# Hybrid backbone on one core: a score product of 128 rows instead of 64, and row statistics issued four chunks together

## The chip, the core and the metric

The kernel runs on one core of a Trainium2 chip. The metric is device time in microseconds (us) of one execution. TensorE (PE) multiplies; its weight loads are shown as an engine of their own, PEld, because they may run beside the products. VectorE (DVE), ScalarE (ACT) and GpSimd (POOL) work element by element, SyncE (SP) starts most transfers. Each engine works through its own queue in order and waits on semaphores for the others. Products write into PSUM, of which this kernel holds five buffers: three wide ones (tag "w", 1024 columns) and two narrow ones (tag "m", 512 columns).

## What is computed

Two layers over 512 latent tokens and 256 context tokens of width 1024. Cut to what matters here:

```python
def rmsnorm(x, g):
    return x * rsqrt(mean(x * x, -1) + EPS) * g

def attend(q, k, v):                       # 4 heads; q, k: 128 columns without and 64 with rotary position
    s = einsum('bqhd,bkhd->bhqk', q, k) * ATTN_SCALE
    return einsum('bhqk,bkhd->bqhd', softmax(s), v)

def layer(xl, xc, ...):                    # latent stream xl, context stream xc
    h = modulate(rmsnorm(x, norm1_g), ...)
    ...                                    # gated MLP, recurrent mixer, attention, concatenated
    x = x + g1 * (concat @ w_out)
    h2 = modulate(rmsnorm(x, norm2_g), ...)
    x = x + g2 * ec_moe(h2)                # 16 experts; each takes its top rows by softmax(h2 @ w_router)

out = rmsnorm(xl, final_norm_g)            # after two layers
```

The context stream gets no output in the second layer, so there the statistics and the experts work on the latent rows alone.

## The kernel before, in words

X holds both streams with the width on the partitions: 8 chunks (k or m) of 128, 512 latent columns (s = 0) and 256 context columns (s = 1). Each layer runs `mixer` (lines 533 to 1036) and then `moe`. The code is written in dependency order; a scheduler sets the order of each engine's queue from priorities when the program is built, so instructions of neighbouring steps interleave.

**Precise products.** A float32 operand that is to be exact is split into a high and a low part in the one-pass format fp32r, and `mm3` (lines 265 to 268) multiplies high by high, low by high and high by low. A product with plain float32 operands runs as two passes (two weight loads and two matmuls in the trace).

**Attention.** Per layer two head pairs p; `scores(h, qt)` computes one tile of 128 queries by 768 keys (256 keys for a context query) in PSUM, in segments of 512 and 256 columns, and for each segment five products: `mm3` on the 128 position-free rows, and two on the rotary rows (lines 963 and 964). `krs[0]` and `krs[1]` hold the high and low part of the rotary key, the 64 rows twice. `qr[h]` holds the high part of head h's rotary query in 64 rows and its low part in the other 64. Line 963 multiplies all 128 rows by `krs[0]`; line 964 takes the 64 high rows alone, by `krs[1]`. Then DVE takes the row maximum (L967), ACT the exponential (L970), DVE the division (L972), PE transposes the result (L985), ACT and DVE split it (L273, L274), and `values` multiplies it by V.

**Row statistics.** The sum of squares over the width is a product with a column of ones, the router's logits one with the router's weights; both have 32 output rows. Chunk k writes PSUM rows 32g to 32g + 31, g = k % 4: one of four column tiles of the PE array. In `Stats.add` (lines 408 to 417), called by `out_tiles` after each update of X (L885), ACT squares the chunk (L411), and PE at once issues two products: router weights by X (L414) and ones by the square (L415), both float32. `Stats.gain` (L423) scales X for the expert rows on ACT. `Ssq` does the same for sums of squares alone (L372): at the start, for the two low-rank norms and at the end of the first layer's experts. `finish` does it for the output (L1184).

**From the statistics to the experts.** `route` copies the sums (L440, L441), turns the four row groups into one column per token (L444), takes the inverse root on DVE, the softmax, and then the top rows of each expert on DVE in rounds of eight (L496, L497, L500), while PE transposes the rows (L477) that ACT scales and SP writes to memory. An indirect gather (L1060) brings the first expert's rows back, and `moe` starts (L1104 in the first layer, L1091 in the second).

**Weights.** `Stream` loads all weights in a fixed order into slots as these come free; a load is issued when the last reader of a slot is done. Six large slots open when the early part of the mixer is over (`early_done`).

Of the kernel before, what the change touches and what calls it, by code (L numbers as in the profile page):

```python
# [7 lines left out]
F32 = mybir.dt.float32  # L8
# [10 lines left out]
TT = T + C  # L19
# [157 lines left out]
def tile_hybrid_backbone(ctx: ExitStack, tc: tile.TileContext, xT, ctxT, cc, cols, fin, w_mod, w_in, w_uq, w_ukv,  # L177
# [181 lines left out]
    class Ssq:  # L359


        def __init__(self, psp, n, nk):
            self.ps, self.n, self.nk = psp.tile([128, 1024], F32, tag="w", name="ssqps"), n, nk

        def add(self, k, src, o, tmp):
            n = src.shape[1]
            sq = tmp()[:, 0]
            act.activation(sq[:, :n], src, AF.Square)
            g = k % 4
            for a in range(0, n, 512):  # L370
                e = min(n, a + 512)
                pe.matmul(self.ps[32 * g:32 * g + 32, o + a:o + e], ones, sq[:, a:e], start=k < 4,  # L372
                          stop=k + 4 >= self.nk)

        def rstd(self, psp, dim, tmp):

# [11 lines left out]
    class Stats:  # L388


        def __init__(self, l, psp, pl):
            self.ps = psp.tile([128, 1024], F32, tag="w", name="stps")
            self.l, self.xa, self.wr = l, ([], []), []
            for s in range(1 if l == L - 1 else 2):
                w = pl.tile([128, KD, 32], F32, tag=f"wr{s}", name=f"wr{s}", bufs=1)
                pool.memset(w, 0.0)
                dve.tensor_mul(w[:, :, :E], wrt[:, l], bcast(A2[l][:, :, s:s + 1], [128, KD, E]))
                self.wr.append(w)
            self.cb = []
            for s in range(len(self.wr)):  # L400
                ps = psp.tile([128, 512], F32, tag="m", name="cb")
                for k in range(KD):
                    pe.matmul(ps[:, :E], bcast(MOD[l][:, SH2 + k, s:s + 1], [128, 128]), wrt[:, l, k], start=k == 0,
                              stop=k == KD - 1)
                self.cb.append(small.tile([128, E], F32, name="cb"))
                dve.tensor_copy(self.cb[s], ps[:, :E])

        def add(self, s, k, tmp, half):
            o, n = SEG[s]
            sq = tmp()[:, 0, :n]  # L410
            act.activation(sq, X[:, k, o:o + n], AF.Square)  # L411
            g = k % 4
            ps = self.ps[32 * g:32 * g + 32, o:o + n]
            pe.matmul(ps, self.wr[s][:, k], X[:, k, o:o + n], start=k < 4, stop=False)  # L414
            pe.matmul(ps, one_e, sq, start=False, stop=k >= 4)  # L415
            if k < KD - 2:
                self.gain(s, k, half)

        def gain(self, s, k, half):

# [112 lines left out]
    def mixer(l, U, psp, rstd, hs):  # L533
# [340 lines left out]
        def out_tiles(key, sub, m0, nm, sg, mh, ml, stats=None):  # L874
            i, wh, wl = S.take(*key, sub)
            nk = wh.shape[1]
            for s, (o, n) in sg:
                for m in range(nm):
                    c = m * 128
                    ps = psp.tile([128, 512], F32, tag="m", name="ops")  # L880
                    for k in range(nk):
                        mm3(ps[:, :n], wh[:, k, c:c + 128], wl[:, k, c:c + 128], mh[k][:, o:o + n], ml[k][:, o:o + n],
                            k == 0, k == nk - 1)
                    xs = X[:, m0 + m, o:o + n]
                    dve.scalar_tensor_tensor(xs, ps[:, :n], MOD[l][:, G1 + m0 + m, s:s + 1], xs, op0=OP.mult,  # L885
                                             op1=OP.add)
# [26 lines left out]
        for p in range(2):  # L913
# [41 lines left out]
            def scores(h, qt):  # L955
                q = slice(qt * 128, (qt + 1) * 128)
                ctx_q = qt * 128 >= T
                ps = psp.tile([128, 1024], F32, tag="w", name="sps")
                r = slice(h * 64, (h + 1) * 64)
                for ko, kn in SEG[1:] if ctx_q else SEG:  # L960
                    c = slice(ko, ko + kn)
                    mm3(ps[:, c], qh[h][:, q], ql[h][:, q], kh[h][:, c], kl[h][:, c], True, False)
                    pe.matmul(ps[:, c], qr[h][:, q], krs[0][:, c], start=False, stop=False)
                    pe.matmul(ps[:, c], qr[h][r, q], krs[1][r, c], start=False, stop=True)
                k0 = T if ctx_q else 0
                mx = small.tile([128, 4], F32, name="mx", bufs=4)
                dve.reduce_max(mx[:, 0:1], ps[:, k0:TT], axis=AX.X)  # L967
# [50 lines left out]
                fills(fl["o1"][p][sub])  # L1018
        rt = [route(l, s, stats, psp, half, tmp, hs) for s in range(len(segs))]
        if full:  # L1020
            next(rt[0])
            Pc = [[scores(h, 4 + i2) for i2 in range(2)] for h in range(2)]
            next(rt[0])
            for h in range(2):
                values(h, 2, Pc[h])
# [3 lines left out]
                out_tiles(("o1", l, 1, 1), sub, 4 * sub, 4, sg_all[1:], ych, ycl, stats)  # L1029
            for _ in rt[0]:  # L1030
                pass
        next(rt[-1])
        mods(fl["route"], psp, ahead=0)
        for _ in rt[-1]:
# [11 lines left out]
    def moe(l, P, psp, last, hs):  # L1046
# [1 line left out]
        M = CAP_L if last else CAP_L + CAP_C  # L1048

        def tmp():  # L1050
            return P.tile([128, 1, T if last else TT], F32, tag="sq" if last else "xst", name="tmp", bufs=3 if last else 4)

        gcol, gidx, sidx, gleft = picks[l]

# [105 lines left out]
        def finish(src):  # L1160
# [3 lines left out]
            slots = [S.raw.pop(0) for _ in range(4)]  # L1164
            xf, ot = [[q.tile([128, 4, 512], F32, tag=t, name=t, bufs=1) for q, t in slots[2 * i:2 * i + 2]]
                      for i in range(2)]
            first = [t[:, c] for t in tm for c in (slice(512), slice(512, 1024))]

            def turn(m, dst):
# [4 lines left out]
            def after(m):  # L1174
# [5 lines left out]
                    act.activation(f, xs, AF.Copy, scale=fint[:, m:m + 1])  # L1180
                else:
                    pool.tensor_scalar(f, xs, fint[:, m:m + 1], None, op0=OP.mult)
                g = m % 4
                pe.matmul(sq_ps[32 * g:32 * g + 32, :512], ones, sq, start=m < 4, stop=m >= 4)  # L1184
                if m < 4:
                    turn(m, first)

# [42 lines left out]
        def flush(e):  # L1230
# [10 lines left out]
            elif e == E - 3:  # L1241
                add_rows(0, lat(E // 2 - 2))
            elif e == E - 1:
                ssq = Ssq(psp, TT, KD)
                for s, src in ((0, lat(E // 2 - 1)), (1, [(YE.pop(("c", e // 4)), 8 + e // 4)])):
                    o, n = SEG[s]
                    add_rows(s, src, lambda m: ssq.add(m, X[:, m, o:o + n], o, tmp))
# [145 lines left out]
```

## Time and profile before

| | |
|---|---|
| median of three runs | 1968.45 us (1968.11 to 1972.2) |
| the profiled execution, its own time | 1967.79 us |
| its span in the trace | 1966.0 us |
| PE busy | 1795.0 us (91%) |
| DVE, ACT, POOL busy | 709.2, 482.1, 80.6 us |
| transfers | 506.52 MB, 258 GB/s on average |

The span lies 1.8 us below the profiled execution's time, and that lies 0.66 us below the median. In a view by windows each row is a stretch of the span with the busy time and count of each engine, the granted PE clock as a share of full speed, the busy share of the transfer engines and GB/s. In the chain of waits each row is a piece of the chain that ended last: its start, its length, engine, tile and line; the recorded chain begins at 468.92 us, so for the first layer's mixer the timeline stands in. A matmul's row in the timeline gives its start and length; consecutive matmuls overlap, so what one costs is read from start to start.

### The profile page before, as it was taken

To read this page: it belongs to the slowest core of one execution; us is meant where nothing else is said; L and a number is where in the kernel's file an instruction comes from. 1 tells how busy PE (TensorE), PEld (TensorE's weight loads), DVE (VectorE), ACT (ScalarE), POOL (GpSimd) and SP (SyncE) were. 2 spreads that over 40 slices of the span, in tenths; PEclk is the share of its full clock that TensorE was granted. 3 is DMA by queue.
4 is the path that set the end of the run, shared out by engine and by line. 5 is a ranking of instruction groups with operands and counts; after the bars stand their busy time and mean duration, and the time that the engine had idled before them with its cause. 6 is when DMAs were issued, how large, how long until landed. Compare 5 with 4: busy or idle time off the path is not lost.

```text
span 1966.0 us, 37614 instructions
## 1 busy us (share of the span) xinstructions
PE 1795.0 (91%) x16777; PEld 1066.6 (54%) x16777; DVE 709.2 (36%) x1479; ACT 482.1 (25%) x839; POOL 80.6 (4%) x95
## 2 busy tenths in 40 slices
PE   7999999996999999999999898999968797887896
PEld 5877778753666566556555686777522232222322
DVE  6456556634111321321322747666331020210213
ACT  4354233442111121121112455244311010010002
POOL 0000000004000000000000000000130000000001
PEclk9999999997999999999999899999979999999998
DMA  9233322226999799799694223322499999999994
GB/s 322 110 131 127 130 87 88 108 93 234 354 386 389 271 395 383 274 389 386 266 366 152 99 108 110 113 77 87 178 330 391 402 398 398 407 389 403 409 409 158
DMA packets 132338, 506.52 MB, mean 258 GB/s; under 512 B 11472, under 2 KB 13392, under 8 KB 124368
## 3 DMA queue, kind: packets, MB, share of 16 engines
q1 hardware_dynamic: 123744, 473.61, 63.1%
q0 software_dynamic: 8288, 30.41, 4.5%
q8 instruction: 132, 2.16, 0.4%
q14 instruction: 30, 0.25, 0.0%
q10 hardware_dynamic: 144, 0.09, 0.0%
HBM read 496.74 MB, written 7.34 MB: 256 GB/s over the span
## 4 chain that ended last, share of the span: by engine, by line
PE 55%; DMA 16%; DVE 3%; ACT 1%; issue 0%; POOL 0%; POOLq 0%; ACTq 0%; DVEq 0%
PE gps L1104 9%; PE ups L1104 9%; PE dps L1104 8%; DMA rawB<-in_w_up 6%; PE cps L1220 4%; PE gps L1091 3%; DMA rawB<-in_w_down 3%; PE ups L1091 2%; DMA rawA<-in_w_down 2%; PE dps L1091 1%; PE inps L266 1%; PE inps L267 1%; PE inps L268 1%; DMA splA<-in_w_up 1%; DMA rawA<-in_w_up 1%; PE ttp L1080 1%
## 5 line engine op out<-in xcount | busy, mean ns | idle before, releaser
L1287 DVE TENSOR_TENSOR hd<-sg,ups 128x768 f32<-128x768 f32 (+1 forms) x32 | 26.3, 821 | 355.5 <-PE ups L1091 202.4
L1104 PE MATMUL dps<-rawB,hdt 128*32 128x256 f32 x1824 | 122.5, 379 | 0.6 <-ACT hdt L1121 0.6
L1104 PE MATMUL gps<-rawB,xst 128*32 128x256 f32 x1584 | 118.4, 380 | 0.0
L266 PE MATMUL inps<-hh,splA 128*128 128x512 f32 (+1 forms) x296 | 106.1, 360 | 5.2 <-ACT splA L133 4.2
L1104 PE MATMUL ups<-rawB,xst 128*32 128x256 f32 x1488 | 105.4, 380 | 0.0
L267 PE MATMUL inps<-hh,splA 128*128 128x512 f32 (+1 forms) x296 | 104.0, 352 | 1.2 <-DVE splA L134 1.2
L268 PE MATMUL inps<-hl,splA 128*128 128x512 f32 (+1 forms) x296 | 103.1, 352 | 0.2 <-DVE hl L601 0.2
L1091 PE MATMUL gps<-rawB,xst 128*64 128x512 f32 x312 | 83.4, 613 | 10.7 <-DMA rawB<-in_w_gate 10.6
L1223 DVE SCALAR_TENSOR_TENSOR X<-cps,mod,X 128x512 f32<-128x512 f32 (+1 forms) x112 | 73.7, 673 | 47.7 <-PE cps L1220 46.6
L1137 ACT ACTIVATE yel<-dps,gcol 64x768 fp32r<-64x768 f32 x16 | 14.3, 894 | 309.6 <-PE dps L1104 309.6
L134 DVE TENSOR_TENSOR splA<-rawA,splA 128x1024 fp32r<-128x1024 f32 (+3 forms) x58 | 65.4, 1138 | 68.3 <-ACT splA L133 67.8
L1091 PE MATMUL ups<-rawB,xst 128*64 128x512 f32 x304 | 76.5, 601 | 14.1 <-DMA rawB<-in_w_up 14.1
L1104 PEld LDWEIGHTS dps<-rawB,hdt 128*32 128x32 f32 x1824 | 67.2, 110 | 39.8 <-ACT hdt L1121 0.8
L1278 ACT ACTIVATE sg<-gps 128x768 f32<-128x768 f32 (+1 forms) x32 | 22.5, 704 | 266.5 <-PE gps L1091 145.3
L1104 PEld LDWEIGHTS gps<-rawB,xst 128*32 128x32 f32 x1584 | 57.7, 110 | 38.8 <-issue 6.9
L133 ACT ACTIVATE splA<-rawA 128x1024 fp32r<-128x1024 f32 (+3 forms) x58 | 56.3, 988 | 91.0 <-PE ops L268 47.0
L885 DVE SCALAR_TENSOR_TENSOR X<-ops,mod,X 128x512 f32<-128x512 f32 (+1 forms) x72 | 47.5, 661 | 82.7 <-PE ops L268 82.7
L1091 PE MATMUL dps<-rawB,hdt 128*64 128x512 f32 x296 | 69.7, 599 | 5.9 <-DMA rawB<-in_w_down 5.9
L1104 PE MATMUL gps<-splA,xst 128*32 128x256 f32 x912 | 74.2, 380 | 0.0
L1104 PEld LDWEIGHTS ups<-rawB,xst 128*32 128x32 f32 x1488 | 54.5, 110 | 32.8 <-PE ttp L1124 1.2
L1138 DVE SCALAR_TENSOR_TENSOR ye<-dps,gcol,ye 64x512 fp32r<-64x512 f32 x32 | 24.0, 750 | 130.0 <-ACT ye L1137 130.0
L1138 DVE SCALAR_TENSOR_TENSOR yel<-dps,gcol,yel 64x768 fp32r<-64x768 f32 x16 | 16.1, 1009 | 149.7 <-ACT yel L1137 149.7
(356 smaller groups left out, 3530.5 us busy)
## 6 DMA issues: line engine op xcount, KB each, us to landing
rawB<-in_w_down SPq DMA_DIRECT2D x75, 1024.0 KB, 14.4
rawB<-in_w_gate SPq DMA_DIRECT2D x65, 1024.0 KB, 15.4
rawB<-in_w_up SPq DMA_DIRECT2D x64, 1024.0 KB, 14.9
rawA<-in_w_mod SPq DMA_DIRECT2D x40, 1024.0 KB, 5.0
splA<-in_w_up SPq DMA_DIRECT2D x30, 1024.0 KB, 12.1
splA<-in_w_down SPq DMA_DIRECT2D x30, 1024.0 KB, 12.8
splA<-in_w_gate SPq DMA_DIRECT2D x29, 1024.0 KB, 13.9
rawA<-in_w_up SPq DMA_DIRECT2D x26, 1024.0 KB, 11.8
```

What stands on the lines that cost most here:

```text
L133: self.nc.scalar.activation(h, src, AF.Copy)
L134: self.nc.vector.tensor_sub(l, src, h.bitcast(F32))
L266: pe.matmul(o, lh, rh, start=start, stop=False)
L267: pe.matmul(o, ll, rh, start=False, stop=False)
L268: return pe.matmul(o, lh, rl, start=False, stop=stop)
L885: dve.scalar_tensor_tensor(xs, ps[:, :n], MOD[l][:, G1 + m0 + m, s:s + 1], xs, op0=OP.mult, op1=OP.add)
L1091: pe.matmul(ps[g * 64:(g + 1) * 64, :512], lhs[:, k], w[:, g * 512:(g + 1) * 512], start=k == 0, stop=k == KD - 1)
L1104: pe.matmul(ps[32 * g:32 * g + 32, to], lhs[:, k, 32 * x:32 * x + 32], w[:, of], start=k == 0, stop=k == KD - 1)
L1138: dve.scalar_tensor_tensor(to[:, 1], ps, gate, to[:, 0].bitcast(F32), op0=OP.mult, op1=OP.subtract)
L1220: pe.matmul(ps[:, :n], y[:, hl, m * 128:(m + 1) * 128], oh[i][:, :n], start=i == 0 and hl == 0, stop=i == len(src) - 1 and hl == y.shape[1 ...
L1223: dve.scalar_tensor_tensor(xs, ps[:, :n], MOD[l][:, G2 + m, s:s + 1], xs, op0=OP.mult, op1=OP.add)
L1287: dve.tensor_mul(HD[e], sg, up)
```

## The change

The last of a score segment's five products takes all 128 rows of `qr[h]` and of `krs[1]` instead of 64 (so the low part of the query meets the low part of the key as well). `Stats.add` only squares and remembers; `emit` issues the products of the remembered chunks, first all with the router's weights, then all with ones, and is called when four are remembered, in `out_tiles` before the next update of X. For the first layer's latent rows one score tile of the context queries is put ahead of the last `emit`. `Ssq` at the end of the first layer's experts and `finish` gather four squares in the same way (the other `Ssq` keep one at a time). The experts' buffer ring for squares in the second layer has 4 places instead of 3.

```diff
         def add(self, k, src, o, tmp):
             ...
             act.activation(sq[:, :n], src, AF.Square)
-            g = k % 4
-            for a in range(0, n, 512):
-                ...
+            self.todo.append((k, sq, o, n))
+            if len(self.todo) == self.batch:
+                for k, sq, o, n in self.todo:
+                    ...
+                self.todo = []
...
         def add(self, s, k, tmp, half):
             ...
             act.activation(sq, X[:, k, o:o + n], AF.Square)
-            g = k % 4
-            ps = self.ps[32 * g:32 * g + 32, o:o + n]
-            pe.matmul(ps, self.wr[s][:, k], X[:, k, o:o + n], start=k < 4, stop=False)
-            pe.matmul(ps, one_e, sq, start=False, stop=k >= 4)
+            self.todo.append((s, k, sq))
             if k < KD - 2:
                 self.gain(s, k, half)
+
+        def emit(self):
+            at = lambda s, k: self.ps[32 * (k % 4):32 * (k % 4) + 32, SEG[s][0]:sum(SEG[s])]
+            for s, k, sq in self.todo:
+                pe.matmul(at(s, k), self.wr[s][:, k], X[:, k, SEG[s][0]:sum(SEG[s])], start=k < 4, stop=False)
+            for s, k, sq in self.todo:
+                pe.matmul(at(s, k), one_e, sq, start=False, stop=k >= 4)
+            self.todo = []
...
+                    if stats and len(stats.todo) == 4:
+                        stats.emit()
                     xs = X[:, m0 + m, o:o + n]
...
-                r = slice(h * 64, (h + 1) * 64)
...
-                    pe.matmul(ps[:, c], qr[h][r, q], krs[1][r, c], start=False, stop=True)
+                    pe.matmul(ps[:, c], qr[h][:, q], krs[1][:, c], start=False, stop=True)
...
+            Pc = [[scores(0, 4)], []]
+            stats.emit()
             next(rt[0])
-            Pc = [[scores(h, 4 + i2) for i2 in range(2)] for h in range(2)]
+            for h, qt in ((0, 5), (1, 4), (1, 5)):
+                Pc[h].append(scores(h, qt))
...
+        stats.emit()
         next(rt[-1])
...
-                g = m % 4
-                pe.matmul(sq_ps[32 * g:32 * g + 32, :512], ones, sq, start=m < 4, stop=m >= 4)
+                sqs.append(sq)
+                if m % 4 == 3:
+                    for g in range(4):
+                        pe.matmul(sq_ps[32 * g:32 * g + 32, :512], ones, sqs.pop(0), start=m == 3, stop=m == 7)
...
-                ssq = Ssq(psp, TT, KD)
+                ssq = Ssq(psp, TT, KD, batch=4)
```

In the attention the order of the queues stays as it was. It moves where statistics are taken. PE, second layer, last output product: `ops` are its products, `stps` the statistics (L414 with the router's weights, L415 with ones; in the changed kernel these are L425 and L427). Before, a piece from its middle:

```order
L414 MATMUL stps<-X,wr_13074 32x512
L268 MATMUL ops<-ycl,splA_12767 128x512
L266 MATMUL ops<-ych,splA_12767 128x512
L415 MATMUL stps<-tmp,one_e 32x512
L267 MATMUL ops<-ych,splA_12767 128x512
L268 MATMUL ops<-ycl,splA_12767 128x512
L266 MATMUL ops<-ych,splA_12767 128x512
L414 MATMUL stps<-X,wr_13074 32x512
```

Now, around the first group:

```order
L268 MATMUL ops<-ycl,splA_12770 128x512
L425 MATMUL stps<-X,wr_13074 32x512 x4
L427 MATMUL stps<-tmp,one_e 32x512 x4
L266 MATMUL ops<-ych,splA_12770 128x512
L267 MATMUL ops<-ych,splA_12770 128x512
```

Single statistics between two or three output products became a block of eight. PE, the end of the same stage, before (`htp` are the transposes of the expert rows, `rpc` is the first step of `route`):

```order
L268 MATMUL ops<-ycl,splA_12770 128x512
L477 MATMUL htp<-ident,xa 128x128 x2
L415 MATMUL stps<-tmp,one_e 32x512
L477 MATMUL htp<-ident,xa 128x128 x6
L414 MATMUL stps<-X,wr_13074 32x512
L477 MATMUL htp<-ident,xa 128x128 x5
L415 MATMUL stps<-tmp,one_e 32x512
L477 MATMUL htp<-ident,xa 128x128 x3
L444 MATMUL rpc<-sel,tmp 128x17 x2
```

and now:

```order
L268 MATMUL ops<-ycl,splA_12770 128x512
L425 MATMUL stps<-X,wr_13074 32x512 x3
L488 MATMUL htp<-ident,xa 128x128
L425 MATMUL stps<-X,wr_13074 32x512
L427 MATMUL stps<-tmp,one_e 32x512 x4
L488 MATMUL htp<-ident,xa 128x128 x4
L455 MATMUL rpc<-sel,tmp 128x17 x2
```

The last group stands behind the last output product, split by one transpose; most transposes moved behind `rpc`. DVE, first layer, top rows of the latent tokens (MAX, MAX_INDEX, MATCH_REPLACE are one round) with the context's updates of X between, before:

```order
L491 COPY tk<-rpt 64x256
L496 MAX gk<-tk 64x8
L497 MAX_INDEX ix<-gk,tk 64x8
L500 MATCH_REPLACE tk<-gk,tk 64x256
L885 SCALAR_TENSOR_TENSOR X<-ops,mod_94,X 128x256
L496 MAX gk<-tk 64x8
L885 SCALAR_TENSOR_TENSOR X<-ops,mod_94,X 128x256
```

and now (the update of X is L898, the rounds are L507, L508, L511):

```order
L502 COPY tk<-rpt 64x256
L507 MAX gk<-tk 64x8
L508 MAX_INDEX ix<-gk,tk 64x8
L511 MATCH_REPLACE tk<-gk,tk 64x256
L507 MAX gk<-tk 64x8
L508 MAX_INDEX ix<-gk,tk 64x8
L511 MATCH_REPLACE tk<-gk,tk 64x256
L898 SCALAR_TENSOR_TENSOR X<-ops,mod_94,X 128x256
```

The first update of X moved one round later; after that they still alternate.

## Rows read from the trace of the kernel before

**Rows 1.** Windows by stage (start:end, length; PE, PEld, DVE, ACT, POOL; clock, DMA, GB/s).

```profile
257.00:309.00 52.00, 48.80 (x423) 36.32 (x422) 35.51 (x85) 25.11 (x55) 0.00 (x0) 0.99 0.35 122
345.00:387.00 42.00, 39.51 (x321) 29.50 (x320) 28.50 (x60) 18.74 (x37) 0.00 (x0) 1.00 0.30 107
...
399.00:429.00 30.00, 29.61 (x86) 11.27 (x85) 8.30 (x13) 11.25 (x19) 0.87 (x1) 0.98 0.22 75
...
441.00:462.00 21.00, 18.82 (x102) 10.56 (x101) 13.24 (x50) 8.81 (x21) 9.57 (x9) 0.99 0.66 230
...
483.00:1071.00 588.00, 586.98 (x9592) 342.97 (x9585) 123.16 (x207) 78.31 (x140) 13.25 (x15) 1.00 0.89 338
...
1072.00:1090.00 18.00, 16.46 (x64) 6.38 (x63) 12.65 (x21) 10.56 (x20) 0.54 (x2) 1.00 0.25 106
...
1272.00:1308.00 36.00, 34.03 (x255) 24.35 (x254) 25.56 (x51) 17.49 (x35) 0.00 (x0) 1.00 0.37 119
1343.00:1387.00 44.00, 40.38 (x275) 30.89 (x276) 28.32 (x59) 19.19 (x40) 0.76 (x1) 0.96 0.20 73
1387.00:1418.00 31.00, 31.00 (x97) 11.84 (x97) 6.43 (x9) 10.45 (x18) 3.51 (x5) 1.00 0.70 271
...
1445.00:1933.00 488.00, 418.90 (x1824) 137.15 (x1820) 72.86 (x117) 42.22 (x78) 12.44 (x14) 1.00 1.02 398
```

**Rows 2.** Line 964, its matmuls: count, ns min/median/max, first and last start, forms.

```profile
L964 PE MATMUL sps<-krs,qr x72: 379/384/502, 263.3 to 1373.9; 64*128 64x256 f32 x40, 64*128 64x512 f32 x32
```

**Rows 3.** Timeline of PE, one score tile of the second layer (start, us, engine, line).

```profile
1372.47 0.40 PE L963 MATMUL sps<-krs,qr 128*128 128x512 f32 x1
1372.80 0.49 PE L964 MATMUL sps<-krs,qr 64*128 64x512 f32 x1
1373.22 0.39 PE L266 MATMUL sps<-kh,qh 128*128 128x256 f32 x1
1373.45 0.28 PE L267 MATMUL sps<-kh,ql 128*128 128x256 f32 x1
1373.56 0.28 PE L268 MATMUL sps<-kl,qh 128*128 128x256 f32 x1
```

**Rows 4.** Chain of waits, second layer, pieces of the output product with statistics.

```profile
1402.27 0.23 PE ops L266
1402.51 0.97 PE stps L415 x2
1403.48 0.43 PE ops L267
...
1404.38 0.97 PE stps L414 x2
1405.36 0.86 PE stps L415 x2
```

**Rows 5.** Timeline, first layer: two statistics products on different column tiles.

```profile
414.32 0.62 PE L415 MATMUL stps<-tmp,one_e 128*32 128x512 f32 x1
414.33 0.62 PE L414 MATMUL stps<-X,wr 128*32 128x512 f32 x1
...
415.31 0.50 PE L267 MATMUL ops<-ych,splA 128*128 128x512 f32 x1
```

**Rows 6.** Chain of waits, first layer's experts: one product on four column tiles.

```profile
539.34 10.36 PE gps L1104 x191
```

**Rows 7.** From the page, part 5: weight loads of such a product (busy, mean ns).

```profile
L1104 PEld LDWEIGHTS gps<-rawB,xst 128*32 128x32 f32 x1584 | 57.7, 110 | 38.8 <-issue 6.9
```

**Rows 8.** Windows in and behind the second layer's last output product.

```profile
1406.00:1414.00 8.00, 8.00 (x25) 3.15 (x24) 2.25 (x3) 2.49 (x4) 0.00 (x0) 1.00 0.00 2
...
1418.00:1445.00 27.00, 8.79 (x114) 6.95 (x114) 17.19 (x76) 7.36 (x15) 14.91 (x15) 0.68 0.57 190
```

**Rows 9.** Windows of 8 us in which PE waits often, or stands nearly still.

```profile
300.00:308.00 8.00, 6.45 (x57) 5.25 (x56) 6.24 (x16) 5.49 (x14) 0.00 (x0) 1.00 0.43 135
...
1437.00:1445.00 8.00, 2.12 (x12) 1.47 (x14) 2.40 (x14) 0.86 (x2) 4.99 (x7) 0.50 0.44 116
```

More of the change, by code (lines that the diff above doesn't have):

```diff
@@ L359, in tile_hybrid_backbone, with __init__ @@
     class Ssq:
-        def __init__(self, psp, n, nk):
+        def __init__(self, psp, n, nk, batch=1):
             self.ps, self.n, self.nk = psp.tile([128, 1024], F32, tag="w", name="ssqps"), n, nk
+            self.batch, self.todo = batch, []
         def add(self, k, src, o, tmp):
@@ L368, in add @@
             act.activation(sq[:, :n], src, AF.Square)
-            g = k % 4
-            for a in range(0, n, 512):
-                e = min(n, a + 512)
-                pe.matmul(self.ps[32 * g:32 * g + 32, o + a:o + e], ones, sq[:, a:e], start=k < 4,
-                          stop=k + 4 >= self.nk)
+            self.todo.append((k, sq, o, n))
+            if len(self.todo) == self.batch:
+                for k, sq, o, n in self.todo:
+                    g = k % 4
+                    for a in range(0, n, 512):
+                        e = min(n, a + 512)
+                        pe.matmul(self.ps[32 * g:32 * g + 32, o + a:o + e], ones, sq[:, a:e], start=k < 4,
+                                  stop=k + 4 >= self.nk)
+                self.todo = []
         def rstd(self, psp, dim, tmp):
@@ L392, in __init__ @@
             self.ps = psp.tile([128, 1024], F32, tag="w", name="stps")
-            self.l, self.xa, self.wr = l, ([], []), []
+            self.l, self.xa, self.wr, self.todo = l, ([], []), [], []
             for s in range(1 if l == L - 1 else 2):
@@ L1050, in tmp @@
         def tmp():
-            return P.tile([128, 1, T if last else TT], F32, tag="sq" if last else "xst", name="tmp", bufs=3 if last else 4)
+            return P.tile([128, 1, T if last else TT], F32, tag="sq" if last else "xst", name="tmp", bufs=4)
         gcol, gidx, sidx, gleft = picks[l]
@@ L1166, in finish @@
                       for i in range(2)]
+            sqs = []
             first = [t[:, c] for t in tm for c in (slice(512), slice(512, 1024))]
```

## The prediction

> **What bounds the kernel now.** First the windows by stage [rows 1]: look at which engine fills each stretch. From 483 to 1071 us, the first layer's experts, PE is busy 586.98 of 588 us; from 1445 to 1933, the second layer's, the transfers have a share of 1.02 and PE waits for weights. Neither stretch holds an edited instruction, so what the change brings must come from the mixers, and each of these two stages then starts earlier by what stands before it. In the attention (257 to 309, 345 to 387, 1272 to 1308, 1343 to 1387) PE is busy 48.80, 39.51, 34.03 and 40.38 us, 163 of 174 us, and DVE 118 us. In the output product with statistics (399 to 429, 1387 to 1418) PE is full and DVE and ACT stay below 12 us each. PE is thus the bound of every stage that the change touches, and the next question is what a PE instruction costs there from start to start.
>
> Second, the single tile [rows 3]. A product of 256 columns is followed by the next after 0.11 us (1373.56 after 1373.45), one of 512 after 0.23, as in the chain, where such a piece is 0.23 long [rows 4]. Around line 964 the steps are longer: 0.33 up to it, 0.42 from it to the next product, and 0.23 for that one, a 256-column product. Over 0.23, 0.23 and 0.11 that is 0.10 + 0.19 + 0.12, about 0.4 us more for one product on 64 rows. There are 72 such products [rows 2].
>
> Third, the chain in the statistics [rows 4]: L415 is a piece of 0.97 us, L414 and L415 in a row 0.97 + 0.86, and the output product behind such a block takes 0.43 instead of 0.23. So the two passes of 512 columns are worth 0.86, entering costs 0.11 and leaving 0.20: a block is 1.17 us, a second product in it 0.86 more.
>
> **The change part by part.** *The score product.* Its own 72 instructions stay; the loss around them goes: 72 x 0.4 = 28 us of PE time at most, 20, 16, 16 and 16 of them in the four attention windows and four among the context's queries. Queue orders stay, so what is late next is softmax: over the four windows PE would need 163 - 27 = 136 us, DVE 118 [rows 1], 87% of PE's, and PE already waits 6.45 busy of 8 us where DVE has 6.24 [rows 9]. So each gap that closes on PE is partly opened again as a wait for DVE and ACT. Bounds: all, 28 us; a third, 9, if DVE's bursts set the pace. I take two thirds, 18.7, since over whole windows PE stays the longer one.
>
> *Statistics of the latent rows, second layer.* Sixteen products stand in 14 blocks now: 14 x 1.17 + 2 x 0.86 = 18.1 us. After, two groups of eight. That a group is cheap rests on column tiles working side by side: at 414.32 an L415 and an L414 on different tiles start 0.01 us apart, and the next output product follows 0.99 later, what one product alone costs [rows 5]; and line 1104, which sends each weight to four column tiles of 256 columns, makes 191 passes in 10.36 us, 54 ns each [rows 6], a quarter of the 0.215 that half of a 512-column pass is. So a group costs 0.11 + 0.86 + 0.86 + 0.20 = 2.03. Two groups are 4.1, and 14.0 us go. The last group comes behind the last output product: it has to wait for that product's update and square, and one transpose splits it; but the lone products that stood there had 13 transposes between them, most of which now come later, beside DVE's work on the root. I let the two cancel, and put one block, 1.2, either way into the bounds.
>
> *Whether this reaches the end.* The weights that the second layer's experts begin with must come in a shorter time. The transfers have a share of 0.70 in 1387 to 1418 [rows 1], with 8 us from 1406 in which they stand still, and 0.57 in the 27 us after it [rows 8]: 9.3 + 11.6, some 21 us idle; 14 fits. The first layer's experts have PE as their bound, so their start moves them whole.
>
> *First layer, latent rows.* The order has 14 blocks too, in one of them two column tiles at once [rows 5]: 14 x 1.17 + 0.86 = 17.2, against 2 x 2.03 = 4.1: 13.1. The score tile put ahead of the last group covers the wait for the last square; it is only moved.
>
> *First layer, context rows.* 256 columns halve the passes: a block is 0.43 + 0.31 = 0.74. Before 14 blocks and one more product, 10.8 us; the order after has three lone products, one group of three and two runs that end in four: six blocks with two second halves, 5.3. PE gives up 5.5 of its 18.82 us in the window 441 to 462, where DVE has 13.24 with the top rows [rows 1]; PE would need 13.3, and the two take turns. I take 4; bounds 1 and 5.5.
>
> *End of the first layer's experts.* Seven blocks instead of ten, some of half width, about 2.7 us of PE's 16.46 in 1072 to 1090; DVE has 12.65 there [rows 1]. I take 2, bounds 0 and 2.7. *Output.* The scheduler spreads the products of `finish` over five blocks instead of six, and one transpose group now stands ahead of four products and waits for POOL: 1 us, bounds -1 and 2, one block each way and a little.
>
> *Sum.* 18.7 + 14.0 + 13.1 + 4 + 2 + 1 = 52.8 us. 1967.8 - 52.8 = 1915.0; the profiled execution lies 0.7 below the median, so 1915.7, rounded to 1916.
>
> *A rule that speaks against it.* The Trainium skill, page "TensorE: Matmul & The Clock Gate", Part 3, "The mechanism", says that a weight load overlaps running products only when its row group differs; column tiles share all rows. What it would make of the time is a rival below.
>
> **The rivals.** *Softmax takes over* (a wait in place of the one removed). If DVE's maxima and splits set the pace, the score term shrinks to 3 to 8 us. For it: the window with 6.24 of 8 us on DVE and 6.45 on PE [rows 9]. Against: DVE's 118 of 174 us [rows 1]. With 5 us: 1929.5, about 1925 to 1933.
>
> *Column tiles run one after another.* Then a group is 8 x 0.86 + 0.31 = 7.2 and only the switches are saved: 18.1 - 14.4 = 3.7, 17.2 - 14.4 = 2.8, little elsewhere; with 18.7 for the scores 26 us, 1942. Against: [rows 5, 6].
>
> *The loads of a group stand open.* Each pass pays its weight load of 110 ns [rows 7]: 96 passes, 10.6 us, 1926. Against: 54 ns per pass at line 1104 [rows 6], half of one load. The rule of the Trainium skill on row groups would give this; the rows of line 1104 differ from it, and the measurement decides.
>
> *The transfers eat the second layer's gain.* If the slots come free no earlier, 14 and that layer's share of the scores are lost, about 23 us: 1939. Against: the idle transfers from 1406 to 1414 [rows 8].
>
> *Slower: PE's clock falls in the attention.* Where PE stood nearly still, 2.12 busy of 8 us, the granted clock was 0.50, its lower level of 1.2 GHz [rows 9]. A PE that waits more often could fall there. Each us of its work at the lower level costs one more; of 136 us of work in the four windows more than 53, some 40%, would have to run so before the kernel is slower than now; with 60% it is 1967.8 - 53 + 82 = 1997. Against: 6.45 busy of 8 us kept 1.00 [rows 9], and I expect at least that share.
>
> **How the numbers follow.** My forecast, scores 12 to 28 and the other terms within their bounds, is 1902 to 1931: chance 0.79. Softmax takes over 0.09; tiles one after another 0.02; open loads 0.03; transfers 0.03; clock 0.04. The range is 1902 to 1932, which holds most of the forecast, half of the softmax case and the open loads, 0.8 or a little over. A measurement of this kernel tells 0.2%, 4 us, from no change. Slower by more than that is the clock case, most of it: 0.03; within it 0.01; faster all else, 0.96.
>
> **What would show it.** Line 964's rows (976 after) would be 128*128 with medians like line 963's, and the steps around it 0.23 and 0.12. The statistics would stand in blocks of eight with some 2 us from start to end; 4 to 7 us would show tiles in turn. The window of the output product in the second layer would shrink from 31 to about 17 us, and the experts of both layers keep their lengths of 588 and 488. The attention windows would be 3 to 7 us shorter each, with more waits of PE for L967, L970 and L273's successors. Wrong would be the forecast if the attention kept its length, if a gather or first weight came late, or if the granted clock in the mixers fell.

## The result, and the profile after

The changed kernel takes 1911.51 us (median of four, 1908.77 to 1914.29), the kernel before 1968.28 beside it: a ratio of 0.9713, 95% interval 0.9696 to 0.973, 56.8 us. A second set of five runs gave 1915.56 us beside 1966.41, 50.9 less by the medians; its recorded ratio is 0.9719 (0.9698 to 0.9739). The profiled execution took 1910.17 us, its span is 1908.4, 57.6 less than the span before.

First the windows of the kernel after, to be set against those of before [rows 1]: start:end, length, busy time and count of PE, PEld, DVE, ACT and POOL, clock, transfer share, GB/s.

```profile
254.00:301.00 47.00, 42.35 (x428) 35.60 (x426) 35.63 (x85) 24.67 (x55) 0.00 (x0) 1.00 0.39 136
...
443.00:1037.00 594.00, 588.65 (x9600) 344.26 (x9600) 123.81 (x211) 78.65 (x141) 19.02 (x22) 0.99 0.88 336
...
1343.00:1360.00 17.00, 16.99 (x87) 10.02 (x85) 6.75 (x10) 10.62 (x18) 3.51 (x5) 1.00 1.02 404
1360.00:1387.00 27.00, 9.01 (x121) 7.57 (x122) 16.55 (x75) 6.87 (x14) 14.65 (x14) 0.74 0.69 240
1387.00:1876.00 489.00, 420.48 (x1826) 137.82 (x1826) 73.18 (x118) 42.56 (x78) 12.71 (x14) 0.99 1.02 398
```

The second layer's output product with statistics, 31 us long before, is 17 us long and just as full. The transfers that stood idle beside it are at 1.02 now, so they did start earlier. Both stages of experts keep their length (first gate product to last down product: 587.5 us in the first layer before and after).

To see where each microsecond went, the trace is cut at marks that both kernels have: first or last starts of a tile's products, as the views by tile give them. (`kps` are the products that make the keys, `pvps` those of `values`; `ops<-ych` is the output product on the attention's result, `gps` the experts' first product, `rpc` the first step of `route`.) The last two columns are two experiments, the new score product alone and the grouped statistics alone.

| stretch | before | after | scores alone | statistics alone |
|---|---|---|---|---|
| start to first score product | 257.6 | 254.7 | 254.2 | 254.7 |
| to first `ops<-ych` (first layer's first head pair) | 55.8 | 50.0 | 49.9 | 55.2 |
| to first `rpc` (second pair, output product, latent statistics) | 115.7 | 97.0 | 110.4 | 101.6 |
| to first `gps` (context rows, route) | 53.7 | 47.3 | 53.1 | 48.3 |
| to last `kps` (first layer's experts, second layer's mixer up to its second pair) | 847.8 | 841.8 | 842.7 | 849.2 |
| to last `rpc` (second pair, output product, statistics) | 88.9 | 70.1 | 84.2 | 74.6 |
| to the end | 546.5 | 547.5 | 547.4 | 548.4 |
| span | 1966.0 | 1908.4 | 1941.9 | 1932.0 |

The two halves add up: in the third line 5.3 and 14.1 make 19.4 against 18.7, in the sixth 4.7 and 14.3 make 19.0 against 18.8. A second trace of the same changed kernel has 95.4 in the third line instead of 97.0, so differences of that size between two traces say nothing. The first line holds no edit; the first `kps` product, 21 us ahead of the scores, starts between 232.1 and 236.8 us in the twelve traces of this study in which nothing ahead of it was edited. Of the 57.6 us some 3 are therefore of that kind.

The timeline of a score tile after (the same place as [rows 3]; start, us, engine, line):

```profile
1328.71 0.39 PE L975 MATMUL sps<-krs,qr 128*128 128x512 f32 x1
1328.95 0.40 PE L976 MATMUL sps<-krs,qr 128*128 128x512 f32 x1
1329.18 0.28 PE L266 MATMUL sps<-kh,qh 128*128 128x256 f32 x1
1329.30 0.28 PE L267 MATMUL sps<-kh,ql 128*128 128x256 f32 x1
```

The steps around the edited product are 0.24, 0.23 and 0.12 us, where they were 0.33, 0.42 and 0.23. The view of that line alone (count; ns min/median/max; first and last start):

```profile
L976 PE MATMUL sps<-krs,qr x72: 276/283/400, 260.2 to 1329.7; 128*128 128x256 f32 x40, 128*128 128x512 f32 x32
```

The median fell from 384 ns [rows 2] to 283, with more rows in the product.

Now a group of statistics, in the timeline of all engines:

```profile
1349.49 0.40 PE L268 MATMUL ops<-ycl,splA 128*128 128x512 f32 x1
1349.82 0.16 PEld L425 LDWEIGHTS stps<-X,wr 128*32 128x32 f32 x8 [0.37 <-issue]
1349.82 1.06 PE L425 MATMUL stps<-X,wr 128*32 128x512 f32 x8
...
1350.27 0.13 PEld L427 LDWEIGHTS stps<-tmp,one_e 128*32 128x32 f32 x4 [0.30 <-ACT tmp L416]
1350.70 1.04 PE L427 MATMUL stps<-tmp,one_e 128*32 128x512 f32 x8
...
1351.67 0.50 PE L266 MATMUL ops<-ych,splA 128*128 128x512 f32 x1
1352.01 0.40 PE L267 MATMUL ops<-ych,splA 128*128 128x512 f32 x1
```

Its sixteen passes (two for each of eight products) stand in two rows of 8. From entry (1349.82) to the next output product (1351.67) it is 1.85 us, plus 0.10 on the way in and 0.11 on the way out: 2.06, where the sum had 2.03. Before, a single product cost 1.17 [rows 4].

The second group of the second layer is not so tidy. The chain of waits after:

```profile
1356.14 0.99 PE stps L425 x6
1357.13 0.26 PE htp L488
1357.39 0.55 PE stps L425
1357.94 0.02 PE stps L427 x3
1357.96 0.41 PE stps L425
1358.37 0.86 PE stps L427 x5
```

Three products go ahead with what is ready, a transpose comes between, and the rest follows: 3.1 us instead of 1.85.

### The profile page after: what moved, and what is told of

The parts are those of the page before. It is cut to its first block, busy times and chain, and to the rows that moved or that the text cites. A ratio compares the mean times of both kernels' runs of the same rounds, so it can differ in the third digit from the quotient of the medians.

```text
span 1908.4 us, 37615 instructions
## 1 busy us (share of the span) xinstructions
PE 1736.6 (91%) x16777; PEld 1059.2 (56%) x16777; DVE 708.3 (37%) x1479; ACT 481.5 (25%) x839; POOL 80.7 (4%) x95
## 4 chain that ended last, share of the span: by engine, by line
PE 55%; DMA 17%; DVE 3%; ACT 2%; issue 1%; POOL 0%; POOLq 0%; ACTq 0%; DVEq 0%
PE gps L1120 9%; PE ups L1120 9%; PE dps L1120 9%; DMA rawB<-in_w_up 6%; PE cps L1239 4%; DMA rawB<-in_w_down 3%; DMA rawA<-in_w_down 3%; PE gps L1107 3%; PE ups L1107 3%; PE dps L1107 1%; PE inps L266 1%; PE inps L267 1%; PE inps L268 1%; DMA splA<-in_w_up 1%; DMA rawA<-in_w_up 1%; PE ttp L1096 1%
## 5 line engine op out<-in xcount | busy, mean ns | idle before, releaser
L1153 ACT ACTIVATE yel<-dps,gcol 64x768 fp32r<-64x768 f32 x16 | 14.3, 894 | 309.6 <-PE dps L1120 309.6
L1120 PEld LDWEIGHTS gps<-rawB,xst 128*32 128x32 f32 x1584 | 57.7, 110 | 38.9 <-issue 6.9
L898 DVE SCALAR_TENSOR_TENSOR X<-ops,mod,X 128x512 f32<-128x512 f32 (+1 forms) x72 | 47.5, 660 | 54.4 <-PE ops L268 54.4
## 6 DMA issues: line engine op xcount, KB each, us to landing
rawB<-in_w_up SPq DMA_DIRECT2D x64, 1024.0 KB, 14.3
rawA<-in_w_up SPq DMA_DIRECT2D x26, 1024.0 KB, 11.8
```

The lines of the kernel that those rows point to most:

```text
L1120: pe.matmul(ps[32 * g:32 * g + 32, to], lhs[:, k, 32 * x:32 * x + 32], w[:, of], start=k == 0, stop=k == KD - 1)
```

## Experiments

### The score product alone

```diff
-                    pe.matmul(ps[:, c], qr[h][r, q], krs[1][r, c], start=False, stop=True)
+                    pe.matmul(ps[:, c], qr[h][:, q], krs[1][:, c], start=False, stop=True)
```

> The kernel before with one line changed: the scores' last product takes all 128 rows. Theory (a product on 64 rows costs 0.4 us around it, and softmax hands part of that back): 72 x 0.4 = 28 us at most, the recorded term is 18.7, and the marks of the changed kernel's trace (its attention windows shorter by about 6, 5 and 10 us, some context tiles beside) point to 20 to 22: 1946 to 1950 us. Rival (softmax takes over): 3 to 8 us, 1960 to 1965. If the two halves of the change help each other, this run and the one with the statistics alone will add up to less than the whole 57 us; the theory has them independent, since they lie in different stretches.

Measured: 1944.71 us against 1966.37, ratio 0.9892 (0.9874 to 0.991), 21.7 us less. Softmax does not take over, but it takes a part back, and matched windows show it. They are the first layer's first head pair (first score product to first `ops<-ych`) and the second layer's second pair (last `kps` to last `pvps`). Before:

```profile
257.60:313.40 55.80, 52.53 (x442) 39.62 (x441) 37.91 (x89) 27.21 (x59) 0.00 (x0) 0.97 0.33 115
1330.60:1386.90 56.30, 52.67 (x346) 41.13 (x345) 34.39 (x72) 23.40 (x49) 0.76 (x1) 0.97 0.20 75
```

the first pair in the run of the next section, the changed kernel with the 64-row product put back:

```profile
254.70:309.90 55.20, 51.45 (x442) 38.16 (x442) 37.91 (x89) 27.05 (x59) 0.00 (x0) 1.00 0.33 116
```

and both in the changed kernel (the run with the scores alone has the same first pair, PE busy 44.68 of 49.9 us):

```profile
254.70:304.70 50.00, 44.82 (x441) 37.39 (x440) 37.92 (x89) 26.66 (x59) 0.00 (x0) 1.00 0.37 128
1290.80:1342.50 51.70, 47.66 (x347) 40.72 (x346) 34.02 (x72) 23.36 (x49) 0.76 (x1) 0.97 0.22 81
```

The first row of before holds more than the edit. For 3.4 us of it the granted clock was at its lower level:

```profile
307.96:311.38 3.42, 3.42 (x18) 3.42 (x17) 1.56 (x4) 1.63 (x4) 0.00 (x0) 0.50 0.30 119
```

The run with the 64-row product put back has no such fall in this stretch and is 0.6 us shorter, so it is the one to compare with. Against it PE's busy time falls by 6.6 us with 20 products, its idle time grows from 3.75 to 5.18 us, and 5.2 reach the end. In the second stretch, with 16 such products and a clock of 0.97 before and after, the busy time falls by 5.0 and the idle time grows by 0.4. Part of the new idle time in the first pair is a wait for softmax (in all, times, longest), where the same wait was 0.6 us before:

```profile
PE sps L266 <- ACT tmp L982: 2.1, 2, 1.5
```

The price itself is read better from start to start, as in [rows 3]: from the product ahead to the second product behind, less 0.2335 us for each 512 columns, the mean step of the output products in the chain. Over the 68 products of the four head pairs these steps lose 27.1 us before and 5.2 in the changed kernel. The difference is 21.8 us, and the run gave 21.7.

### The statistics alone

The changed kernel with the 64-row product put back.

> The changed kernel with the 64-row score product put back, so that the grouped statistics stand alone. Theory: 14.0 + 13.1 + 4 + 2 + 1 = 34 us below the kernel before, 1934 us; the marks of the changed kernel's trace (13.3, 14.0, about 5, 0.3, 0) say 33 to 35. Rival (column tiles one after another): 8 us, 1960. Rival (each pass pays its weight load): about 24 us, 1944. Rival (transfers take the second layer's part): 20 us, 1948.

Measured: 1934.32 us, ratio 0.9841 (0.9821 to 0.9862), 32.0 us less than before. The table splits it: 14.1 for the first layer's latent rows, 5.4 for the context rows, 14.3 for the second layer; the other stretches move by -2.9 to +1.9 us and cancel. None of the three rivals comes near.

### Is it the entry, or the product on 64 rows?

Three runs ask what the 0.4 us is paid for. In the kernel before, the 64-row product twice in a row; in the changed kernel, the 128-row product twice; and in the kernel before, the two 64-row products of a tile put next to each other.

```diff
-                for ko, kn in SEG[1:] if ctx_q else SEG:
-                    c = slice(ko, ko + kn)
+                cs = [slice(ko, ko + kn) for ko, kn in (SEG[1:] if ctx_q else SEG)]
+                for c in cs:
                     mm3(...)
                     pe.matmul(ps[:, c], qr[h][:, q], krs[0][:, c], start=False, stop=False)
+                for c in cs:
                     pe.matmul(ps[:, c], qr[h][r, q], krs[1][r, c], start=False, stop=True)
```

> The kernel before with the score product on 64 rows issued twice in a row, so that this part of the scores counts double. Theory (the price lies in going from 128 to 64 rows and back, once each, however many such products stand in a row): only the product's own time is added, 32 x 0.23 + 40 x 0.11 = 11.8 us of TensorE, of which 8 to 12 reach the end: 1975 to 1980 us. Rival (each product on 64 rows costs 0.4 us more by itself): 28 us on top, 40 in all, of which 32 to 40 reach the end: 1998 to 2008.

> The changed kernel with the score product on 128 rows issued twice in a row, so that this part counts double: the counterpart of the run with two products on 64 rows. Both theories: 11.8 us of TensorE are added, and because softmax leaves TensorE some idle time in the attention now, 6 to 11 of them reach the end: 1917 to 1923 us against 1911.5. If the same 72 products cost 11 us or more here, TensorE is still the bound of the attention; if 4 or less, softmax has become it.

> The kernel before with the score products of a tile in another order: the products of both blocks of keys on 128 rows first, then the two on 64 rows next to each other, so that a tile of 768 keys is entered and left once instead of twice. All products and results stay. Theory (price per entry and exit): 32 of 72 such pairs go, 32 x 0.4 = 12.8 us at most, by the share of 21.7 in 28 that the full-row product gave, 10 us: 1957 us. Rival (price per product): no change, 1966 to 1968.

Measured: two on 64 rows 1973.13 us, ratio 1.0036 (1.0021 to 1.0052) to the kernel before, 7.0 us more, just under the 1975 to 1980 expected; two on 128 rows 1922.25, 0.9772 (0.9756 to 0.9789), 7 to 11 more than the two sets of the changed kernel; paired 1954.00, 0.9936 (0.9922 to 0.9951), 12.1 us less than before without any product left out, where 10 were expected. So the price is of going to 64 rows and back, and a second such product in the row costs only itself. The timeline of the run with two:

```profile
1377.60 0.40 PE L963 MATMUL sps<-krs,qr 128*128 128x512 f32 x1
1377.92 0.50 PE L964 MATMUL sps<-krs,qr 64*128 64x512 f32 x1
1378.26 0.39 PE L965 MATMUL sps<-krs,qr 64*128 64x512 f32 x1
1378.59 0.39 PE L266 MATMUL sps<-kh,qh 128*128 128x256 f32 x1
1378.81 0.28 PE L267 MATMUL sps<-kh,ql 128*128 128x256 f32 x1
```

From L963 to the second product behind the visit it is 1.21 us with two and 0.98 with one [rows 3]: 0.23 more, the own time of a 512-column product. In the paired run both stand in one visit:

```profile
1362.81 0.28 PE L963 MATMUL sps<-krs,qr 128*128 128x256 f32 x1
1363.01 0.61 PE L965 MATMUL sps<-krs,qr 64*128 64x512 f32 x2
1363.56 0.33 PE L986 MATMUL tps<-ident,tmp 128*128 128x128 f32 x1
```

32 visits are saved, so the 12.1 us are 0.38 each. The Trainium skill, page "TensorEngine Tiling (Array Packing)", section "Key Properties", says that changing the tiling mode, not just the tile, drains TensorE. The traces agree in that each change costs time: some 0.4 us for a visit of 64-row products, some 0.3 for one of 32-column tiles [rows 4]. That a drain is what takes this time, no run shows.

### Are the four column tiles what makes a group cheap?

Two runs. In the first, the two products of a chunk stand next to each other again, on the same column tile, within the group of eight:

```diff
             for s, k, sq in self.todo:
                 pe.matmul(at(s, k), self.wr[s][:, k], X[...], start=k < 4, stop=False)
-            for s, k, sq in self.todo:
                 pe.matmul(at(s, k), one_e, sq, start=False, stop=k >= 4)
```

> The changed kernel with the two products of a chunk put next to each other again, still four chunks in one group: the column tiles go a, a, b, b, c, c, d, d instead of a, b, c, d, a, b, c, d. The number of groups and of switches stays. Theory (a group is cheap because neighbours on different column tiles run side by side, and two on one tile wait for each other): five passes of 0.86 us one behind another instead of two, 2.6 us more for each of the four groups of 512 columns, 10.3 us, and about 2 us for the context rows: 1922 to 1925 us against 1911.5. Rival (a group is cheap because it is entered and left once, whatever the tiles): no change, 1911 to 1913. The second layer's last group stands in one piece here, without a transpose inside, which may give 1 us back.

Measured: 1912.73 us, ratio 0.9727 (0.9708 to 0.9746): no different from the changed kernel. My theory had foretold 10 us, so as I had put it, it fell. But the rival that went with this run (the tiles do not matter) was not shown either, since the chain of this run says that the group is as short as before:

```profile
1350.98 1.01 PE stps L425 x8
1351.99 0.86 PE stps L426 x8
1352.85 0.43 PE ops L266
```

Either a product that waits for its own tile does not hold up the next one for another tile, or tiles play no part. (That the queue did hold the products in the new order shows in their starts: products on neighbouring tiles start 13 ns apart in this run and 7 ns apart in the changed kernel.) The second run takes the other tiles away: all chunks on the first column tile, the sums then read from 32 rows.

```diff
-            at = lambda s, k: self.ps[32 * (k % 4):32 * (k % 4) + 32, SEG[s][0]:sum(SEG[s])]
+            at = lambda s, k: self.ps[:32, SEG[s][0]:sum(SEG[s])]
             ...
```

> The changed kernel with all chunks of the row statistics on the first column tile instead of four; the groups of eight products, their order and their number of switches stay, and the row sums then read 32 rows instead of 128. Theory (the tiles of a group work side by side, and the queue in front of each runs ahead, which is why putting the two products of a chunk next to each other cost nothing): a group of 512 columns is 8 x 0.86 = 6.9 us instead of 1.7, 5.2 more for each of four groups, 20.6 us, and up to 5 for the two groups of the context rows: 1932 to 1937 us. Rival (a group is cheap because it is entered and left once, and products follow each other in a group at the same pace on any tile): no change, 1911 to 1913.

Measured: 1930.65 us, ratio 0.9836 (0.9815 to 0.9857), some 15 to 19 us above the two sets of the changed kernel and just under the 1932 to 1937 expected: the context rows, for which up to 5 us had been allowed, lost nothing (47.5 us from the first `rpc` to the first `gps` product, against 47.3 and 47.7). The chain:

```profile
1358.86 3.55 PE stps L425 x8
1362.41 3.43 PE stps L427 x8
1365.84 0.43 PE ops L266
```

A group on one tile takes 6.98 us, 5.1 more than on four, and four of them make 20.5. The two stretches with latent statistics agree: 107.1 and 79.4 us here, 95.4 to 97.0 and 70.1 in the changed kernel, 19.4 to 21.0 more together. So the passes do run side by side, and the gain of the statistics has two parts: on one tile, some 70% of the 28.4 us that the four groups gain is lost by these traces.

### The sums at the ends

The changed kernel with the squares at the end of the first layer's experts and in `finish` summed one by one again.

> The changed kernel with the root-mean-square sums at the end of the first layer's experts and in the output stage issued one by one again. Recorded terms: 2 and 1 us, so 3 us slower than the changed kernel, 1914.5. The marks of its trace (0.3 and 0) say no difference, 1911 to 1912, because those products wait there for VectorE's updates and not for TensorE.

Measured: 1914.02 us, ratio 0.973 (0.9709 to 0.9751), which lies between the two sets of the changed kernel: no difference that runs can tell. From the last down product of the first layer to the first `ssqc` product (the first step from the sums to the root) it is 20.5 us before and in this run, 20.0 and 21.9 in the two profiled runs of the changed kernel. The chain of waits has the first sums (`ssqps`) and that step, before:

```profile
1076.06 1.61 PE ssqps L372 x4
...
1090.80 0.83 PE ssqc L384 x6
```

and in the changed kernel:

```profile
1044.73 1.77 PE ssqps L376 x8
...
1056.46 0.83 PE ssqc L389 x6
```

The last down product starts at 1070.32 before and at 1036.48 after. So the first sums come 5.7 us behind it before, and 8.2 after, because a group has to wait until DVE has updated four chunks (5.7 in all five traces without this group, 8.2 to 8.3 in all nine with it). From there to the root it is 14.7 us before and 11.7 to 13.7 in the nine. PE does save time in the groups, 1 to 3 us, but 2.5 are lost at the start. At the output, from the last `cps` product (which adds the experts' rows to X) to the end of the span, it is 18.8 us before, 18.4 in this run and 19.5 in both traces of the changed kernel: there the group costs a little.

### Fewer visits elsewhere

If every visit to another shape has its price, others can be gathered too. One kernel holds the modulation's products (line 318, four column tiles, 16 products in a piece, put as filling between other work) back until two pieces go out together. The second adds two more: the statistics' group is led by the product that waits longest, so that all eight go in one piece, and in the first layer's experts two chunks of context rows share a PSUM tile.

```diff
             i, w, _ = S.take("mod", l, c, t, 0, ahead=ahead)
             ...
+            if t == 0:
+                mod_ps["w"] = i, ws
+                return
+            late = [mod_ps.pop("w")]
             ...
```

> The changed kernel with the products of the modulation (line 318, 16 products of 128 columns on four column tiles in a piece, put between other work) issued two pieces together, 32 products in a row; 18 pieces fewer in the order. Theory (every piece on another shape costs its entry and exit, 0.10 + 0.11 us by the steps around such a piece in the changed kernel's trace, whatever the work): 18 x 0.2 to 0.3, 3.6 to 5.4 us, 1906 to 1908 us. Rival (only the 64-row product and the pieces of 512 columns had such a price): no change, 1911 to 1913. Rival (a weight held back for its partner keeps a slot, and the loads behind it come late): slower by some us.

> The run with the modulation's pieces together, and two more of the same kind: a group of the row statistics is led by the product that waits longest, so that all eight stand in one piece (6 pieces instead of 11), and the rows of the context from two neighbouring chunks share a PSUM tile when the first layer's experts add them (6 pieces fewer). Theory: 3.6 to 5.4 us as there, 5 x 0.3 = 1.5 and 6 x 0.2 = 1.2 more: 6 to 8 us below the changed kernel, 1903.5 to 1905.5 us. Rival (the waits for the squares and for VectorE set the pace in these places): the same as the run with the modulation alone.

> The changed kernel itself, on the same chip as the two kernels with fewer pieces, since the differences asked for are a few us: 1911 to 1913 us.

Measured: 1962.61 us for the modulation in pairs, ratio to the kernel before 0.9972 (0.9959 to 0.9986); 1957.80 with all three, 0.9955 (0.9939 to 0.9972); 1915.56 for the changed kernel beside them. Nearly the whole gain was gone, by a mechanism that I had named without a price. The first `kps` product starts at 262.7 us instead of 233.3, and the last at 1339.9 instead of 1290.8. The window from 110 us up to the first `kps` product, in pairs:

```profile
110.00:263.00 153.00, 135.23 (x1017) 106.62 (x1015) 80.94 (x129) 56.87 (x70) 0.00 (x0) 0.93 0.30 109
```

and in the changed kernel:

```profile
110.00:234.00 124.00, 118.47 (x913) 93.63 (x906) 78.06 (x124) 54.51 (x67) 0.00 (x0) 0.99 0.34 123
```

PE's idle time grew from 5.5 to 17.8 us, and its granted clock fell from 0.99 to 0.93. What the weight loads waited for on SP's queue in these windows (in all, times, longest), in pairs:

```profile
SPq L100 <- PE modps L325: 110.0, 11, 18.7
```

and in the changed kernel:

```profile
SPq L100 <- PE modps L318: 66.6, 9, 14.8
```

In the window of the pairs PE waited, among others, for weights that were not yet split into high and low parts (`splA`), which the other window does not have:

```profile
PE ops L266 <- ACT splA L133: 7.7, 2, 4.6
...
PE kps L266 <- ACT splA L133: 3.1, 1, 3.1
```

A load starts when the products that read its slot are done; with one piece held back, its slot is held, and the next weights come late. Whether this is the cause was asked of one more kernel: all three groupings, but the modulation held only inside the attention.

```diff
+                        mod_ps["hold"] = n_ + 1 < n_fill
                         fills(1)
+                        mod_ps["hold"] = False
                         ...
```

> The run with all three groupings, but with the modulation's pieces held together only inside the attention, where the weights have time; in the input projections each piece goes out when its weight is there, as in the changed kernel. 16 pieces fewer than there (5 of the modulation, 5 of the statistics, 6 of the experts' context rows). Theory (the 47 us were lost because a weight held back for its partner keeps a slot of the weight stream where the input projections wait for weights; the grouping itself gains its entries and exits): the first product of kps is back at 232 to 237 us, and the time is 5 x 0.25 + 5 x 0.3 + 6 x 0.2 = 4 us below the changed kernel, 1907 to 1912 us. Rival (32 products of the modulation in a row, or the leading product of the statistics, are themselves what costs): 1930 us or more.

Measured: 1906.75 us (1906.18 to 1916.68), ratio 0.97 (0.9672 to 0.9729); the first `kps` product is back at 233.7 us, and so is the wait of the weight loads in the window up to it:

```profile
SPq L100 <- PE modps L326: 64.9, 9, 14.8
```

So the groups outside the input projections are not what cost 47 us, holding pieces back in the input projections is. That it acts through the slot is what the rows of waits say; no run held the pieces back with a slot to spare. That this kernel beats the changed one is not settled by its runs, whose interval covers 0.9713 and 0.9719. In the trace, the stretch from the first `rpc` to the first `gps` product, where the context rows' groups now stand in one piece, is 45.1 us; it is 47.3 to 47.7 in the two traces of the changed kernel and in the two of its variants with chunks in turn and with the sums at the ends one by one. This is no gain by itself, since five more score products now stand ahead of the first `rpc` product: from the first score product to the first `gps` product it is 192.6 us, and 192.9 to 194.3 in those four. Its second group of the second layer, in the chain:

```profile
1353.30 1.60 PE htp L499 x13
1354.90 0.55 PE stps L433
...
1355.46 0.41 PE stps L433
...
1355.89 0.96 PE stps L438 x8
```

It stands in one piece of 1.95 us (1354.90 to 1356.85), with the transposes ahead of it.

## Why the prediction was right, point by point

**PE is the bound in the mixers.** Right. Two more products on 128 rows per tile cost 7 to 11 us of the 11.8 that PE needs for them, even after the change.

**0.4 us for each visit, 28 us at most, two thirds of it at the end.** The price held: read from start to start, 59 of the 68 products in the four head pairs lose 0.38 to 0.50 us and nine, each with a modulation product right behind it, 0.23 to 0.31; the paired run gives 0.38 per visit. (72 x 0.4 is 28.8, not 28, which changes nothing.) The share was sized too low: 21.7 us, not 18.7. The step that failed is the one from "softmax is late next" to a third lost: 5.2 of 27.1 us came back, a fifth, and 3.7 of them at four places. What was read from 8 us in which PE waits often [rows 9] was not typical of a stage.

**Latent statistics, 14.0 and 13.1 us.** 14.3 and 14.1, taken alone. The group of eight costs 2.06 us for 2.03. That a split second group and fewer lone blocks cancel was a guess that came out within 0.3 us in the second layer, by luck, since the split group takes 3.1 us and not 1.85.

**Context rows, 4 of at most 5.5.** 5.4: PE gave up all that it could; the turn-taking with DVE that I had allowed for took nothing. This term was mis-sized by 1.4.

**The ends, 2 and 1 us.** Nothing that the times can tell, in the trace 0.5 and -0.7. The first term left out a wait: PE saved 1 to 3 us where 2.7 had been counted, but the first group starts 2.5 us later, because it needs four of DVE's updates. The row of this stretch, PE 16.46 and DVE 12.65 of 18 us [rows 1], did not show that. The second term had the wrong sign. Terms too low by 3.0, 1.4 and 1.3 and these too high by some 3 leave 2.7 us (the first is a difference of medians, the others come from traces, so this is rough), and the stretch ahead of any edit brought 2.9: 5.6, about the 4.8 by which the span fell more than the sum of 52.8. That the errors had different signs was luck.

**Whether it reaches the end.** Right: the transfers went from a share of 0.70 to 1.02 in the output product's window, and the second layer's experts start 57.7 us earlier.

**The rivals.** Softmax took a part, not the whole. Tiles in turn: refuted by the run on one tile. Open weight loads: the group's row at 1350.27 shows four loads while products of the same rows run, and the next row of products starts at 1350.70 without a gap. The Trainium skill, page "TensorE: Matmul & The Clock Gate", Part 3, "The mechanism", has in its list of what overlaps a load only if its row group differs (the paragraph above that list also names the background weight buffer). The measurement differs from the list, with 1.85 us for 16 passes whose loads of 106 to 110 ns would be 1.7 on top. Transfers: they moved along. The clock: 0.97 to 1.00 in the two attention stretches, as before or higher.

## What to carry to other kernels

Read the cost of a small matmul from the start of the product before it to the second start behind it: a product that takes other rows or column tiles than its neighbours pays for the change of shape both ways, and a wider product with more work in it, or several of the same shape in a row, can be cheaper. Gather such products where what they read is ready anyway. Before holding one back to fill a group, ask which buffer it holds, who waits for that buffer, and how much later the first product of the group can start.

## What was not expected of the hardware

Two products on one column tile, one behind the other, did not hold up the products for other tiles that stood behind them in the queue: eight products in the order a, a, b, b, c, c, d, d took 1.87 us, in the order a, b, c, d, a, b, c, d 1.85. In a group the weight loads run ahead of the products (1350.27 for 1350.70), but at its entry the load starts 0.33 us after the last product ahead started, not earlier, and 0.37 us of the load engine's idle time there is put down to issue: the load is not pulled ahead across a change of shape. That, more than the array itself, may be what a visit pays for; this is a guess, and no run here tells the two apart.
